# Score passes of the first query block between second value products, and key blocks 2 and 3 through one transposed tile

## The chip, the cores and the metric

One Trainium2 chip, one core. The metric is the device time of one execution in microseconds, the median of several runs. All arithmetic of the attention runs in float32, where each operand that a product needs exactly is split in a high and a low half.

## The reference

A decoder trunk of two layers on 512 tokens (plus 16 learned meta tokens in front), width 1024. Each layer has one combined input projection and two parallel mixers, a causal pooling and a latent attention with 8 heads, both gated and added:

```python
h = rmsnorm(h_res, norm_gain[l])
proj = h @ w_in[l]
u_pool, z_pool, c_q, c_kv, k_rope, z_mla, g_pool, g_mla = jnp.split(proj, IN_SPLIT_POINTS, axis=-1)
y_pool = (pool_mix(u_pool, pool_w_group[l], pool_scale[l]) * jax.nn.silu(z_pool)) @ pool_w_up[l]
o_mla = mla(c_q, c_kv, k_rope, pos, q_a_norm_gain[l], kv_a_norm_gain[l], w_q_b[l], w_kv_b[l],
            q_norm_gain[l], k_norm_gain[l])
y_mla = (o_mla * jax.nn.silu(z_mla)) @ mla_w_up[l]
merged = jax.nn.sigmoid(g_pool) * y_pool + jax.nn.sigmoid(g_mla) * y_mla
h_res = h_res + merged @ w_out[l]
```

Inside `mla`, each head computes for each block of 128 queries `softmax(q k^T * scale)` over all keys up to the block's end, and the product of these weights with the values.

## The kernel before

Activations lie transposed: features on the 128 partitions, the 528 tokens along the free axis. A plan lists every weight product of both layers in order ("Gemm"); a generator (`stream`) emits them pass by pass. Each product is three TensorE passes (`mm3`, lines 180 to 182): high by high, high by low, low by high. In layer 0 a product covers the tokens in two segments of 264 columns, in layer 1 (`self.last`), where the meta tokens are no longer wanted, in one of 512.

The attention of a layer is emitted in between. `gap()` emits so many nanoseconds (`FILL`) of the plan's passes as filler, and the loop over the 8 heads goes round like this: score passes of query blocks 1, 2 and a part of 3 of head h; gap; first part of the value products of head h-1 (key blocks 0 and 1); gap; score passes of the rest of block 3 and of block 0, row minima, exponentials and normalisation of head h; gap; `prep` of head h+1, second part of the value products of head h-1 (key blocks 2 and 3); gap.

A scheduler then sets each engine's own order when the kernel is built: among the instructions whose inputs it holds for ready, those emitted first go first. On the chip each engine follows that order; semaphores make it wait where an input is late. So filler passes that were emitted later can stand between two steps of a head whose inputs were not ready together.

The steps of one head, in the order in which one feeds the next:

- `prep`: the keys are scaled (DVE line 742, POOL line 743), and split into `kh` (ACT, line 271) and `kl` (DVE, line 272).
- `scores(i)`: `mm3` of query block i, 128 columns of weights from `qh` or `ql`, with 144 columns (block 0), 272 (1), 400 (2), and 240 and 288 (3, in two parts) of keys, into PSUM tiles "S".
- `top` (line 774): scale, mask and row minimum on DVE. `expo` (line 781): the exponential on ACT with row sum. Then the reciprocal of the row sums on DVE (line 813), and on POOL the normalisation of the weights of all four blocks (lines 818 and 820).
- `pv`, per key block j: transposes of the normalised weights (line 839), split into `th` (ACT, line 271) and `tl` (DVE, line 272), then two products into the PSUM tile "o": the wide one (line 844, 128 columns of weights with the value's high and low half, `th` moving) and the low one (line 845, 64 columns of weights, `tl` moving). Each has 512 - 128 j columns. Odd heads also turn the weights of the meta tokens (line 850).
- `part2` (line 868): the meta tokens' share, and the gate.

Of the kernel before, what the change touches and what calls it, by code (L numbers as in the profile page):

```python
# [9 lines left out]
F32 = mybir.dt.float32  # L10
F32R = mybir.dt.float32r
BF16 = mybir.dt.bfloat16
I32 = mybir.dt.int32
AF = mybir.ActivationFunctionType
# [4 lines left out]
P = 128  # L19
DEPTH = 2  # L20
D = 1024
SEQ = 512
NM = 16
# [4 lines left out]
H = 8  # L28
# [43 lines left out]
def trunk(ctx, tc, xT, xrow, mrow, pos, win, wkr, wqb, wkb, wvb, wgr, wpu, wmu, wout, gains, const, yT):  # L72
    nc = tc.nc
    pe, act, dve, gp, sp = nc.tensor, nc.scalar, nc.vector, nc.gpsimd, nc.sync
# [5 lines left out]
    sm = ctx.enter_context(tc.tile_pool(name="sm", bufs=1))  # L80
    dp = ctx.enter_context(tc.tile_pool(name="dp", bufs=1, space=bass.MemoryType.DRAM))
    pp = ctx.enter_context(tc.tile_pool(name="pp", bufs=1, space=bass.MemoryType.PSUM))
# [3 lines left out]
    def nm(s):  # L86
        uid[0] += 1
        return f"{s}_{uid[0]}"
# [10 lines left out]
    def mmt():  # L99
        return pp.tile([P, 512], F32, tag="mm", name=nm("mm"), bufs=4)  # L100

    def sct():
        return pp.tile([P, 512], F32, tag="S", name=nm("S"), bufs=3)
# [27 lines left out]
    ident = cst[:, C_ID:C_ID + P]  # L131
# [27 lines left out]
    vt = cp.tile([P, 4, H, P], F32R, name="vt")  # L159
# [109 lines left out]

    def split(hi, lo, src, a, b):  # L270
        act.activation(hi[:, a:b], src, AF.Copy)  # L271
        dve.tensor_sub(lo[:, a:b], src, hi[:, a:b].bitcast(F32))  # L272

    def behind(ins, other):
        tc.add_manual_dep(ins.ins, other.ins.name,
                          mybir.DependencyInfo(mybir.DependencyClass.Sync, mybir.DependencyReason.DATA))
# [32 lines left out]
    class Layer:  # L309
# [449 lines left out]
        def head(self, h, kq, prev):  # L759
            kh, kl, qh, ql = kq  # L760
            odd = h % 2
            nqs = self.nqs
            pa = slot("pa", bufs=2, w=416)
            pb = slot(f"cq{8 + odd}")
            pc = slot(f"cq{10 + odd}")
            bia = sm.tile([P, 5], F32, tag="bia", name=nm("bia"), bufs=2)
            rs = sm.tile([P, 5], F32, tag="rs", name=nm("rs"), bufs=2)

            def scores(i, out, a, b):
                q0 = NM + P * i  # L770
                mm3(out, qh[:, q0:q0 + P], ql[:, q0:q0 + P], kh[:, a:b], kl[:, a:b], True, True)

            def top(i, c, sv, mask):
                dve.tensor_tensor_reduce(out=sv, in0=sv, in1=mask, scale=nqs[:, i, h:h + 1], scalar=3e38,  # L774
                                         op0=ALU.add, op1=ALU.min, accum_out=bia[:, c:c + 1])

            def causal(n):
                return maskw[:, 512 - n:]

            def expo(i, c, sv, pv):  # L780
                act.activation(pv, sv, AF.Exp, scale=-1.0, bias=bia[:, i:i + 1], accum_out=rs[:, c:c + 1])  # L781

            pt = [pa[:, 0:144], pa[:, 144:416], pb[:, 0:400], pc[:, 0:T]]
            sa = sct()
            s1, s3 = sa[:, 0:272], sa[:, 272:272 + SPL]
            scores(1, s1, 0, 272)
            scores(3, s3, 0, SPL)
            top(1, 1, s1, causal(272))
            top(3, 4, s3, maskw[:, 0:SPL])
            sb = sct()  # L790
            s2 = sb[:, 0:400]
            scores(2, s2, 0, 400)
            if not self.last:
                mm3(sb[0:NM, 400:416], qh[:, 0:NM], ql[:, 0:NM], kh[:, 0:NM], kl[:, 0:NM], True, True)
                dve.tensor_add(self.smeta[:, h, :], sb[0:NM, 400:416], cst[0:NM, C_MM:C_MM + NM])
            top(2, 2, s2, causal(400))
            expo(1, 1, s1, pt[1])
            expo(2, 2, s2, pt[2])
            self.gap()
            self.pv(prev, (0, 1))  # L800
            self.gap()
            sc = sct()
            s0, s4 = sc[:, 0:144], sc[:, 144:144 + T - SPL]
            scores(3, s4, SPL, T)
            scores(0, s0, 0, 144)
            top(3, 3, s4, causal(T - SPL))
            top(0, 0, s0, causal(144))
            dve.tensor_tensor(out=bia[:, 3:4], in0=bia[:, 3:4], in1=bia[:, 4:5], op=ALU.min)  # L808
            expo(3, 4, s3, pt[3][:, 0:SPL])
            expo(3, 3, s4, pt[3][:, SPL:T])  # L810
            expo(0, 0, s0, pt[0])
            dve.tensor_add(rs[:, 3:4], rs[:, 3:4], rs[:, 4:5])
            dve.reciprocal(rs[:, 0:4], rs[:, 0:4])  # L813
            if odd == 0:
                self.pm = sm.tile([P, 4, 32], F32, tag="pm", name=nm("pm"), bufs=2)
            for i in range(4):
                n = pt[i].shape[1]
                gp.tensor_mul(self.pm[:, i, 16 * odd:16 * odd + 16], pt[i][:, 0:NM],  # L818
                              rs[:, i:i + 1].to_broadcast([P, NM]))
                gp.tensor_mul(pt[i][:, NM:], pt[i][:, NM:], rs[:, i:i + 1].to_broadcast([P, n - NM]))  # L820
            return h, pt, self.pm

        def pv(self, prev, js):
            if prev is None:
                return
            h, pt, pm = prev
            p, odd = h // 2, h % 2
            if js[0] == 0:
                self.o = sct() if h == H - 1 else pp.tile([P, 512], F32, tag="o", name=nm("o"), bufs=1)
            ops = self.o  # L830
            if odd == 1 and js[0] == 0:
                self.pmr = sm.tile([P, 4, 2, 32], F32R, tag="pmr", name=nm("pmr"))
                act.activation(self.pmr[:, :, 0, :], pm, AF.Copy)
                dve.tensor_sub(self.pmr[:, :, 1, :], pm, self.pmr[:, :, 0, :].bitcast(F32))
            for j in js:
                n = SEQ - P * j
                tr = mmt()
                for i in range(j, 4):
                    pe.transpose(tr[:, P * (i - j):P * (i - j + 1)], pt[i][:, NM + P * j:NM + P * (j + 1)], ident)  # L839
                th = tp.tile([P, W], F32R, tag="th", name=nm("th"), bufs=2)  # L840
                tl = tp.tile([P, W], F32R, tag="tl", name=nm("tl"), bufs=2)
                split(th, tl, tr[:, :n], 0, n)
                out = ops[:, P * j:512]
                pe.matmul(out, vt[:, j, h, :], th[:, :n], start=j == 0, stop=j == 3)  # L844
                pe.matmul(out[0:64], vt[:, j, h, 0:64], tl[:, :n], start=False, stop=j == 3, skip_group_check=True)  # L845
            if js[-1] != 3:
                if odd == 1:
                    tr = sct() if h == H - 1 else mmt()
                    for i in range(4):
                        pe.matmul(tr[0:64, P * i:P * (i + 1)], self.pmr[:, i].rearrange("p a b -> p (a b)"), identr,  # L850
                                  start=True, stop=True)
                    self.mt = slot("racc", F32R)
                    act.activation(self.mt[0:64, 0:512], tr[0:64, :], AF.Copy)
                    act.activation(self.mt[64:96, 0:512], tr[0:32, :], AF.Copy)
                return
            if odd == 0:
                self.op = tmp()
            n0, m0 = (64, 0) if odd else (0, 64)
            op = self.op[n0:n0 + 64, NM:T]
            act.activation(op, ops[m0:m0 + 64, :], AF.Copy)  # L860
            dve.tensor_add(op, ops[n0:n0 + 64, :], op)
            if odd == 1:
                op = self.op
                mt = self.mt

                def part2():
                    th, m = mt, mmt()
                    pe.matmul(m, self.vb[:, P * p:P * (p + 1)], th[0:96, 0:512], start=True, stop=True)  # L868
                    self.ogs[p] = (slot(f"q{p}", F32R), slot(f"kn{p}", F32R))
                    f = op[:, NM:T]  # L870
                    dve.tensor_add(f, m, f)
                    dve.tensor_mul(f, f, self.zms[p][:, NM:T])
                    split(*self.ogs[p], f, NM, T)

                after((3 if p == 3 else 2) * LAG, part2)
# [141 lines left out]
        def go(self, nxt):  # L1017
# [42 lines left out]
            prev = None  # L1060
            for h in range(H):
                kn_ = self.head(h, kq, prev)
                self.gap()
                if h + 1 < H:
                    kq = self.prep(h + 1)
                self.pv(prev, (2, 3))
                prev = kn_
                self.gap()
            fill_now(1300)
            self.pv(prev, (0, 1))  # L1070
            if not self.last:
                self.meta_queries()
            fill_now(2600)
            self.pv(prev, (2, 3))
            up("gm7")
            flush()
            if not self.last:
# [84 lines left out]
```

## Time and profile before

| | |
|---|---|
| median of three runs | 778.08 us (778.04 to 778.8) |
| the profiled execution | 778.45 us, of which the span is 776.6 us |
| TensorE busy | 771.7 us, 5251 passes |
| weight loads | 702.8 us, 5251 |
| DVE, ACT, POOL busy | 534.3, 414.2, 206.9 us |
| mean granted TensorE clock | 0.999 |
| attention of layer 0 | about 173 to 323 us into the span (first score pass to last value product) |
| attention of layer 1 | about 565 to 706 us into the span |

In the profile, PE is a TensorE pass and PEld its weight load. A row of the timeline has the start, the duration, the engine, the line, the operation, the tile written and those read, the weights' rows and columns, and the moving operand's partitions and columns. TensorE's passes overlap in its pipeline, so their durations add up to more than the time.

### The profile page before, as it was taken

What the parts mean: (1) busy time and instruction counts of PE and PEld (TensorE: products, weight loads), DVE (VectorE), ACT (ScalarE), POOL (GpSimd) and SP (SyncE); (2) the same over time, 40 slices, a digit from 0 to 9 for tenths busy, and PEclk for the clock granted to TensorE, in tenths of its full rate; (3) what the DMA queues carried; (4) which work ended last, traced back from release to release, by engine and by line L of the source; (5) the groups of instructions that cost most, each with busy time, mean ns of one, the idle gap of its engine ahead of it and who ended that gap; (6) DMA issues with size and microseconds to landing.
All of it is one profiled execution on the core that took longest, in us unless ns stands there. A gap on an engine that the chain in (4) does not pass through costs nothing.

```text
span 776.6 us, 14527 instructions
## 1 busy us (share of the span) xinstructions
PE 771.7 (99%) x5251; PEld 702.8 (90%) x5251; DVE 534.3 (69%) x1155; ACT 414.2 (53%) x930; POOL 206.9 (27%) x265
## 2 busy tenths in 40 slices
PE   9999999999999999999999999999999999999998
PEld 8999899999999999999997898887788888888887
DVE  5588688357788977785466486774577888765932
ACT  6755656545666665633354365455446666654420
POOL 1026404012334242052120263030132433420500
PEclk9999999999999999999999999999999999999999
DMA  8533234433222222325643332244232332122372
GB/s 284 164 112 98 74 92 123 123 96 103 92 82 87 79 67 71 96 82 153 188 134 91 110 89 87 79 132 141 76 123 89 96 89 89 59 79 68 108 241 85
DMA packets 54932, 84.04 MB, mean 108 GB/s; under 512 B 10007, under 2 KB 18583, under 8 KB 54861
## 3 DMA queue, kind: packets, MB, share of 16 engines
q1 hardware_dynamic: 54716, 82.86, 35.2%
q8 instruction: 41, 0.67, 0.4%
q14 instruction: 31, 0.25, 0.1%
q10 hardware_dynamic: 144, 0.26, 0.1%
HBM read 76.68 MB, written 4.29 MB: 104 GB/s over the span
## 4 chain that ended last, share of the span: by engine, by line
PE 99%; DMA 1%; SPq 0%; ACT 0%; DVE 0%; issue 0%
PE mm L180 29%; PE mm L182 29%; PE mm L181 29%; PE mm L839 2%; PE S L181 2%; PE S L182 2%; PE S L180 2%; PE o L844 1%; PE o L845 1%; PE S L498 1%; DMA raw<-win 1%; PE S L462 0%; PE mm L868 0%; PE mm L387 0%; PE mm L850 0%; PE S L845 0%
## 5 line engine op out<-in xcount | busy, mean ns | idle before, releaser
L180 PE MATMUL mm<-hh,whi 128*128 128x264 f32 (+2 forms) x1096 | 345.4, 317 | 0.3 <-ACT whi L175 0.3
L181 PE MATMUL mm<-hl,whi 128*128 128x264 f32 (+2 forms) x1096 | 343.2, 314 | 0.0
L182 PE MATMUL mm<-hh,wlo 128*128 128x264 f32 (+2 forms) x1096 | 342.5, 314 | 0.0
L176 DVE TENSOR_TENSOR wlo<-raw,whi 128x512 fp32r<-128x512 f32 (+2 forms) x251 | 181.4, 726 | 103.7 <-ACT whi L175 101.4
L175 ACT ACTIVATE whi<-raw 128x512 fp32r<-128x512 f32 (+2 forms) x251 | 150.5, 603 | 178.9 <-PE mm L181 134.3
L180 PEld LDWEIGHTS mm<-hh,whi 128*128 128x128 f32 x1096 | 205.5, 188 | 13.6 <-ACT whi L175 0.5
L181 PEld LDWEIGHTS mm<-hl,whi 128*128 128x128 f32 x1096 | 206.1, 188 | 12.0
L182 PEld LDWEIGHTS mm<-hh,wlo 128*128 128x128 f32 x1096 | 205.2, 188 | 12.2
L743 POOL TENSOR_TENSOR tmp<-kp,bc 64x528 f32<-64x528 f32 x16 | 24.8, 1552 | 103.7 <-issue 53.5
L818 POOL TENSOR_TENSOR pm<-pa,rs 128x16 f32<-128x16 f32 x32 | 11.7, 365 | 148.6 <-DVE rs L813 148.6
L604 POOL TENSOR_TENSOR racc<-racc,tmp 128x264 f32<-128x264 f32 (+1 forms) x15 | 14.3, 957 | 113.9 <-ACT tmp L603 113.9
L928 POOL TENSOR_TENSOR tmp<-tmp,xb 128x264 f32<-128x264 f32 (+1 forms) x24 | 26.7, 1134 | 57.7 <-DVE tmp L926 55.5
L774 DVE CUSTOM_DVE_ANT_0 S<-S,maskw,nqs 128x272 f32<-128x272 f32 (+4 forms) x80 | 38.4, 498 | 2.2 <-PE S L182 1.9
L180 PE MATMUL mm<-u,whi 128*128 128x264 f32 (+1 forms) x108 | 35.1, 325 | 0.0
L182 PE MATMUL mm<-u,wlo 128*128 128x264 f32 (+1 forms) x108 | 34.7, 321 | 0.0
L180 PE MATMUL mm<-cq,whi 128*128 128x264 f32 (+1 forms) x108 | 34.6, 321 | 0.0
L181 PE MATMUL mm<-cq,whi 128*128 128x264 f32 (+1 forms) x108 | 34.6, 321 | 0.0
L182 PE MATMUL mm<-cq,wlo 128*128 128x264 f32 (+1 forms) x108 | 34.6, 320 | 0.0
L272 DVE TENSOR_TENSOR tl<-mm,th 128x512 fp32r<-128x512 f32 (+1 forms) x64 | 29.3, 482 | 7.0 <-ACT th L271 6.0
L781 ACT ACTIVATE cq<-S,bia 128x400 f32<-128x400 f32 (+2 forms) x48 | 24.5, 515 | 17.8 <-DVE bia L808 8.8
L820 POOL TENSOR_TENSOR cq<-cq,rs 128x384 f32<-128x384 f32 (+1 forms) x32 | 33.5, 1047 | 0.0
L271 ACT ACTIVATE th<-mm 128x512 fp32r<-128x512 f32 (+1 forms) x64 | 25.4, 434 | 6.5 <-PE mm L839 5.9
(271 smaller groups left out, 1370.8 us busy)
## 6 DMA issues: line engine op xcount, KB each, us to landing
raw<-win SPq DMA_DIRECT2D x143, 256.0 KB, 2.6
raw<-wout SPq DMA_DIRECT2D x32, 256.0 KB, 3.0
bc<-kdr SPq DMA_DIRECT2D x16, 264.0 KB, 3.1
raw<-wpu SPq DMA_DIRECT2D x16, 256.0 KB, 2.9
raw<-wmu SPq DMA_DIRECT2D x16, 256.0 KB, 2.7
raw<-wqb SPq DMA_DIRECT2D x12, 256.0 KB, 3.0
xb<-xT SPq DMA_DIRECT2D x8, 264.0 KB, 5.5
tmp<-xT SPq DMA_DIRECT2D x16, 132.0 KB, 3.4
```

Source lines behind the costliest of these rows:

```text
L175: act.activation(hi[:, :n], raw[:, :n], AF.Copy)
L176: dve.tensor_sub(lo[:, :n], raw[:, :n], hi[:, :n].bitcast(F32))
L180: pe.matmul(out, wh, xh, start=start, stop=False)
L181: pe.matmul(out, wh, xl, start=False, stop=False)
L182: newest[0] = pe.matmul(out, wl, xh, start=False, stop=stop)
L271: act.activation(hi[:, a:b], src, AF.Copy)
L272: dve.tensor_sub(lo[:, a:b], src, hi[:, a:b].bitcast(F32))
L743: gp.tensor_mul(kf[r0:r0 + 64, :], self.kp[r0:r0 + 64, :], bc[r0:r0 + 64, :])]
L774: dve.tensor_tensor_reduce(out=sv, in0=sv, in1=mask, scale=nqs[:, i, h:h + 1], scalar=3e38, op0=ALU.add, op1=ALU.min, accum_out=bia[:, c:c ...
L781: act.activation(pv, sv, AF.Exp, scale=-1.0, bias=bia[:, i:i + 1], accum_out=rs[:, c:c + 1])
L820: gp.tensor_mul(pt[i][:, NM:], pt[i][:, NM:], rs[:, i:i + 1].to_broadcast([P, n - NM]))
L928: gp.tensor_add(t[:, :b - a], t[:, :b - a], self.am[m][:, a:b])
```

## The change

In layer 0, for every head that has a previous one, the three score passes of query block 0 are no longer emitted in a run. They go to `pv` as "hosts" of the second part of the previous head's value products. `pv` now has three parts: part 0 turns and splits key blocks 0 and 1; part 1, one gap later, has their products, with the score passes in between, and the low product of block 0 in two halves of 256 columns; part 2 has key blocks 2 and 3. In layer 1 parts 0 and 1 are emitted one behind the other, and the last head of each layer does its products in part 0; there the score passes of block 0 stay in a run.

In part 2, in both layers, the transposes of key blocks 2 and 3 go into one PSUM tile of 384 columns with one split, and the products are ordered: wide 2, wide 3, low 3, low 2.

`follow` sets an order between two instructions of an engine without a semaphore. `behind` makes an instruction wait: the first and third host wait for the low half (`tl`) of block 0's and block 1's tile, and the wide product of block 3 for that of the shared tile.

```diff
     def split(hi, lo, src, a, b):
         act.activation(hi[:, a:b], src, AF.Copy)
-        dve.tensor_sub(lo[:, a:b], src, hi[:, a:b].bitcast(F32))
+        return dve.tensor_sub(lo[:, a:b], src, hi[:, a:b].bitcast(F32))
+
+    def follow(ins, other):
+        tc.add_manual_dep(ins.ins, other.ins.name,
+                          mybir.DependencyInfo(mybir.DependencyClass.NoSync, mybir.DependencyReason.SCHED_ONLY))
...
-            self.pv(prev, (0, 1))
+            self.pv(prev, 0)
+            if self.last:
+                self.pv(prev, 1)
             self.gap()
             sc = sct()
             s0, s4 = sc[:, 0:144], sc[:, 144:144 + T - SPL]
             scores(3, s4, SPL, T)
-            scores(0, s0, 0, 144)
+            if prev is None or self.last:
+                scores(0, s0, 0, 144)
+            else:
+                q0 = slice(NM, NM + P)
+                self.pv(prev, 1, [lambda k=k, q=q, x=x: pe.matmul(s0, q[:, q0], x[:, 0:144], start=k == 0, stop=k == 2)
+                                  for k, (q, x) in enumerate(((qh, kh), (qh, kl), (ql, kh)))])
...
+            def turned(js):
+                tr, c = mmt(), 0
+                for j in js:
+                    for i in range(j, 4):
+                        pe.transpose(tr[:, c:c + P], pt[i][:, NM + P * j:NM + P * (j + 1)], ident)
+                        c += P
                 th = tp.tile([P, W], F32R, tag="th", name=nm("th"), bufs=2)
                 tl = tp.tile([P, W], F32R, tag="tl", name=nm("tl"), bufs=2)
-                split(th, tl, tr[:, :n], 0, n)
-                out = ops[:, P * j:512]
-                pe.matmul(out, vt[:, j, h, :], th[:, :n], start=j == 0, stop=j == 3)
-                pe.matmul(out[0:64], vt[:, j, h, 0:64], tl[:, :n], start=False, stop=j == 3, skip_group_check=True)
-            if js[-1] != 3:
+                return th, tl, split(th, tl, tr[:, :c], 0, c)
+
+            def ready(t, fn):
+                ins = fn()
+                behind(ins, t[2])
+                return ins
+
+            def both(j, t, c):
+                n = SEQ - P * j
+                return pe.matmul(ops[:, P * j:512], vt[:, j, h, :], t[0][:, c:c + n], start=j == 0, stop=j == 3)
+
+            def low(j, t, c, a=0, b=512):
+                a, b = max(a, P * j), min(b, 512)
+                return pe.matmul(ops[0:64, a:b], vt[:, j, h, 0:64], t[1][:, c + a - P * j:c + b - P * j],
+                                 start=False, stop=j == 3, skip_group_check=True)
+
+            def chain(*fns):
+                last = None
+                for fn in fns:
+                    ins = fn()
+                    if last is not None:
+                        follow(ins, last)
+                    last = ins
+
+            if part == 0:
+                self.t01 = [turned((0,)), turned((1,))]
+            if part == (0 if final else 1):
+                t0, t1 = self.t01
+                if hosts:
+                    chain(lambda: both(0, t0, 0), lambda: ready(t0, hosts[0]), lambda: low(0, t0, 0, 0, 256), hosts[1],
+                          lambda: low(0, t0, 0, 256, 512))
+                    chain(lambda: both(1, t1, 0), lambda: ready(t1, hosts[2]), lambda: low(1, t1, 0))
+                else:
+                    for j, t in enumerate(self.t01):
+                        both(j, t, 0)
+                        low(j, t, 0)
...
+            if part < 2:
                 return
+            t = turned((2, 3))
+            chain(lambda: both(2, t, 0), lambda: ready(t, lambda: both(3, t, 256)), lambda: low(3, t, 256), lambda: low(2, t, 0))
...
-                self.pv(prev, (2, 3))
+                self.pv(prev, 2)
...
-            self.pv(prev, (0, 1))
+            self.pv(prev, 0)
...
-            self.pv(prev, (2, 3))
+            self.pv(prev, 2)
```

More of the change, by code (lines that the diff above doesn't have):

```diff
@@ L821, in head, with pv @@
             return h, pt, self.pm
-        def pv(self, prev, js):
+        def pv(self, prev, part, hosts=()):
             if prev is None:
@@ L827, in pv @@
             p, odd = h // 2, h % 2
-            if js[0] == 0:
-                self.o = sct() if h == H - 1 else pp.tile([P, 512], F32, tag="o", name=nm("o"), bufs=1)
-            ops = self.o
[L831 to L839, printed above, removed]
+            final = h == H - 1
@@ new lines, in pv @@
+            if part == 0:
+                self.o = sct() if final else pp.tile([P, 512], F32, tag="o", name=nm("o"), bufs=1)
+                if odd == 1:
+                    self.pmr = sm.tile([P, 4, 2, 32], F32R, tag="pmr", name=nm("pmr"))
+                    act.activation(self.pmr[:, :, 0, :], pm, AF.Copy)
+                    dve.tensor_sub(self.pmr[:, :, 1, :], pm, self.pmr[:, :, 0, :].bitcast(F32))
+            ops = self.o
+            def turned(js):
[4 more added lines that the diff above has]
+                        c += P
@@ new lines, in chain @@
+            def chain(*fns):
[5 more added lines that the diff above has]
+                    last = ins
+            if part == 0:
+                self.t01 = [turned((0,)), turned((1,))]
[9 more added lines that the diff above has]
+                        low(j, t, 0)
@@ L847, in pv @@
                 if odd == 1:
-                    tr = sct() if h == H - 1 else mmt()
+                    tr = sct() if final else mmt()
                     for i in range(4):
```

## The prediction

> **What bounds the kernel now.** I read the page first (span, clock, chain), then TensorE's passes in order of time inside the attention stretch of layer 0, then its weight loads over the same microseconds, and last the vector, scalar and GpSimd engines between one head and the next.
>
> ```profile
> span 776.6 us, 14527 instructions
> PE 771.7 (99%) x5251; PEld 702.8 (90%) x5251; DVE 534.3 (69%) x1155; ACT 414.2 (53%) x930; POOL 206.9 (27%) x265
> PEclk9999999999999999999999999999999999999999
> PE 99%; DMA 1%; SPq 0%; ACT 0%; DVE 0%; issue 0%
> ```
>
> TensorE is busy in 99% of the span, the chain that ends last is TensorE for 99% of its length, and the granted clock is full in every slice. So the time is the sum of what TensorE's passes cost, one behind the other, and an edit is worth what it changes in that sum, plus any wait that it brings to TensorE. The durations in these rows are no prices, because passes overlap in the pipeline: the price of a pass is the distance from its start to the next start. Here are the three score passes of query block 0 (144 columns) of one head, between wide passes:
>
> ```profile
> 211.88 0.28 PE L182 MATMUL mm<-hh,wlo 128*128 128x264 f32 x1
> 212.00 0.23 PE L180 MATMUL S<-kh,qhl 128*128 128x144 f32 x1
> 212.06 0.28 PE L181 MATMUL S<-kl,qhl 128*128 128x144 f32 x1
> 212.17 0.28 PE L182 MATMUL S<-kh,qhl 128*128 128x144 f32 x1
> 212.29 0.33 PE L180 MATMUL mm<-hh,whi 128*128 128x264 f32 x1
> 212.45 0.29 PE L181 MATMUL mm<-hl,whi 128*128 128x264 f32 x1
> 212.58 0.39 PE L844 MATMUL o<-th,vt 128*128 128x512 f32 x1
> 212.81 0.28 PE L182 MATMUL mm<-hh,wlo 128*128 128x264 f32 x1
> ```
>
> A 264-column pass costs 0.12 us (211.88 to 212.00) and a 512-column pass 0.23 (212.58 to 212.81). The difference, 0.11 us for 248 columns, is 0.444 ns a column. By that a 144-column pass should cost 0.12 - 120 x 0.000444 = 0.067 us and a 128-column pass 0.06. But the second and third score passes take 0.11 and 0.12, and the wide pass behind them 0.16 (212.29 to 212.45) in place of 0.12. The weight loads of the same stretch say why:
>
> ```profile
> 212.00 0.19 PEld L181 LDWEIGHTS S<-kl,qhl 128*128 128x128 f32 x1
> 212.11 0.19 PEld L182 LDWEIGHTS S<-kh,qhl 128*128 128x128 f32 x1
> 212.22 0.19 PEld L180 LDWEIGHTS mm<-hh,whi 128*128 128x128 f32 x1
> 212.33 0.19 PEld L181 LDWEIGHTS mm<-hl,whi 128*128 128x128 f32 x1
> ```
>
> The load for the next pass starts when the present pass starts (212.00 in both views), and loads of 128 columns follow each other at 0.11 us. So a pass costs the larger of its own stream and the load of the pass behind it. A 264-column pass (0.12) covers that load; a 144-column pass (0.067) does not. Three short passes in a row take 0.33 us of loads (212.00 to 212.33) for 0.20 of streams: 0.13 us a head lost.
>
> The same loss, smaller, sits at the last value products (key block 3, 128 columns):
>
> ```profile
> 222.46 0.28 PE L845 MATMUL o<-tl,vt 128*64 128x256 f32 x1
> 222.58 0.22 PE L844 MATMUL o<-th,vt 128*128 128x128 f32 x1
> 222.64 0.22 PE L845 MATMUL o<-tl,vt 128*64 128x128 f32 x1
> 222.70 0.34 PE L181 MATMUL mm<-hl,whi 128*128 128x264 f32 x1
> 222.87 0.28 PE L182 MATMUL mm<-hh,wlo 128*128 128x264 f32 x1
> ```
>
> ```profile
> 222.64 0.19 PEld L181 LDWEIGHTS mm<-hl,whi 128*128 128x128 f32 x1
> 222.75 0.19 PEld L182 LDWEIGHTS mm<-hh,wlo 128*128 128x128 f32 x1
> ```
>
> The wide product (222.58) is followed by the low product after 0.06 us: it is not delayed, because the low product loads only 64 columns, and 0.06 covers that. The low product itself (222.64) is followed by a pass with 128 columns of weights. The next loads are 0.11 apart, and the pass behind takes 0.17 in place of 0.12. So 0.05 us is lost behind every 128-column product whose successor loads 128 columns.
>
> **The change part by part.**
>
> *Score passes of query block 0 between value products.* This holds in layer 0 for heads 1 to 7; head 0 and all of layer 1 keep the run of three. The new order is: wide product of block 0 (512 columns), score pass, low product's first half (256), score pass, low product's second half (256); then wide product of block 1 (384), score pass, low product (384). Each score pass's 128-column load lies under a pass of 256 columns or more (at least 0.117 us by the slope, against 0.11), and behind each score pass (0.067) comes a 64-column load, which 0.06 covers. All 0.13 us are won back: 7 x 0.13 = 0.91 us.
>
> ```profile
> 282.17 0.28 PE L182 MATMUL S<-kh,qhl 128*128 128x144 f32 x1
> 282.29 0.40 PE L850 MATMUL mm<-identr,pmr 128*64 128x128 f32 x4
> ```
>
> In one of the seven heads the third pass already has a pass with 64 columns of weights behind it, so I take 0.04 (0.11 less 0.067) off: 0.87.
>
> The split low product adds one pass a head. Two of 256 columns cost 2 x 0.117 = 0.234 against 0.23, some 0.005 us, in all 0.04. Net of this part: 0.83 us.
>
> The interleaved run itself is not in the trace. Its bounds are that every score pass still pays 0.11 (nothing won, 0.04 lost) and that it costs 0.06, the shortest start-to-start of the rows above (another 21 x 0.007 = 0.15 won). I take the covered price of 0.067, since the row that is nearest, a 128-column product in front of a 64-column load, shows exactly its stream.
>
> *Key blocks 2 and 3 through one tile.* Both layers, all heads. The order becomes wide block 2 (256), wide block 3 (128), low block 3 (128), low block 2 (256). Behind both 128-column products there is now a 64-column load, and the last pass, 256 columns, covers a load of 128.
>
> ```profile
> L845 PE MATMUL o<-tl,vt 128*64 128x128 f32 x14 | 3.2, 229 | 0.0
> L845 PE MATMUL S<-tl,vt 128*64 128x128 f32 x2 | 0.4, 221 | 0.0
> ```
>
> ```profile
> 204.56 0.22 PE L844 MATMUL o<-th,vt 128*128 128x128 f32 x1
> 204.62 0.33 PE L180 MATMUL mm<-hh,whi 128*128 128x264 f32 x1
> ...
> 706.32 0.22 PE L844 MATMUL S<-th,vt 128*128 128x128 f32 x1
> ```
>
> All 16 low products of block 3 lose 0.05 now. In five heads (the first and the last are shown) the wide product loses it too, because another pass stands between it and its low product. 21 x 0.05 = 1.05 us. If the new pairs were pulled apart by wide passes, all 32 would lose it, 0.55 us more than now; if the gain is not a stall's doing it cannot be above 1.05. I take 1.05, as 11 of the 16 pairs stand together today and the new wait on the split's second half stands in front of the pair, not inside it.
>
> *What is moved at no price.* The transposes are the same in number and place. The products of blocks 0 and 1 stand one filler stretch later, with the plan's filler passes in between, so the cover is the wide passes that the rows above show on both sides; were they used up, TensorE would wait for the split tiles. Sixteen copies and sixteen subtractions of splits are saved on engines that the chain does not name. No DMA is issued or moved, and neither SP's nor POOL's queue is passed.
>
> *The added wait.* The first and the third hosted score pass wait for the vector engine's low half of the tile. The low product behind each needs that half anyway, so TensorE gets no new wait of its own, but the score of block 0 comes later. Behind it stand the row minimum on the vector engine, the exponentials, and the normalisation on GpSimd. What that does is the second rival.
>
> *A rule against this.* The rows show a load starting with the previous pass, both with all 128 rows. The Trainium skill, "TensorE: Matmul & The Clock Gate", Part 3 (What overlaps and what doesn't), says that weight loads overlap running matmuls only where the row group differs. By that rule no order of these passes could hide a load; the loads at 212.00 and 222.64 contradict it here.
>
> The sum: 0.83 + 1.05 = 1.88, so 1.9 us less. The profiled execution (778.45, of which 776.6 is the span) would become 776.6. It stands 0.37 above the median of the three runs, 778.08, and the forecast goes from the median: **776.2 us**. A difference of 0.2% (1.56 us) is about what a measurement of this kernel can tell from no change.
>
> **The rivals.**
>
> *First: the groups do not stay together.* If wide passes slip in behind each score pass and behind each product of block 3, 0.87 of the gain is gone, the 0.04 of the split remain, and block 3 costs 0.55 more: 778.1 + 0.6 = 778.7. Against it: in the rows above passes that become ready together are issued together. For it: five pairs are apart today.
>
> *Second, slower: the later score reaches the next head.* In one head of the trace the whole chain runs without slack:
>
> ```profile
> 215.14 0.34 PE L845 MATMUL o<-tl,vt 128*64 128x384 f32 x1
> ...
> 223.37 0.58 PE L180 MATMUL S<-kh,qhl 128*128 128x272 f32 x2
> ```
>
> ```profile
> 212.06 1.14 DVE L272 TENSOR_TENSOR tl<-mm,th 128x512 fp32r<-128x512 f32 x2
> ...
> 213.72 0.38 DVE L774 CUSTOM_DVE_ANT_0 S<-S,maskw,nqs 128x144 f32<-128x144 f32 x1
> ```
>
> ```profile
> 219.57 1.59 POOL L820 TENSOR_TENSOR cq<-cq,rs 128x512 f32<-128x512 f32 x1
> 221.12 1.52 POOL L743 TENSOR_TENSOR tmp<-kp,bc 64x528 f32<-64x528 f32 x1
> 232.92 1.81 POOL L743 TENSOR_TENSOR tmp<-kp,bc 64x528 f32<-64x528 f32 x1 [10.28 <-issue]
> ...
> 241.44 1.04 POOL L820 TENSOR_TENSOR cq<-cq,rs 128x512 f32<-128x512 f32 x1
> ```
>
> ```profile
> 222.68 0.64 ACT L271 ACTIVATE kh<-tmp 128x528 fp32r<-128x528 f32 x1 [3.41 <-POOL tmp L743]
> ```
>
> The low halves are done by 213.20, but TensorE comes to the low product of block 1 only at 215.14, since its order is fixed. The third hosted score pass stands just ahead of that product, so the minimum over block 0 starts at about 215.14 + 0.28 = 215.42 (the row's place plus a score pass's 0.28 to its end) and not at 213.72: 1.7 us later. GpSimd normalises this head and only then makes the next head's key (221.12, straight behind 219.57). The scalar engine then finishes it at 223.32, and TensorE reads it at 223.37. There are 0.05 us of slack, so TensorE would wait 1.65 us. In the next head GpSimd makes the key ahead of the normalisation (232.92 before 241.44), and the delay reaches no score pass. One such head costs 1.65 and leaves 776.2 + 1.65 = 777.85, within 0.2%. Three cost 4.95: **781.1 us**. It decides from the third head on, since (1.88 + 1.56) / 1.65 is 2.1.
>
> *Third: loads cannot be hidden.* If each load ran by itself, the order of passes would be worth nothing, and the seven added passes would cost a 64-column load (0.06) more each: 778.1 + 7 x 0.06 = 778.5. This is what the rule quoted above would give. The loads that start with a running pass speak against it.
>
> **How the numbers follow.** Forecast as summed, up to a few tenths lost to single pulled-apart pairs: 0.55, with its own range 775.8 to 776.5. One or two heads waiting: 0.17 (777.85 for one). Groups pulled apart: 0.06 (778.7). Loads not hidden: 0.02 (778.5). Three heads or more waiting: 0.20 (781.1). Faster by over 0.2% is the first, 0.55; within it the next three, 0.25; slower the last, 0.20. The low end, 775.8, is the forecast less the 0.15 of the lower bound and 0.25 for the spread of the runs (from 778.04 to 778.08 and 778.8); the high end, 778.8, takes in the rivals within 0.2% and leaves out the 0.20 above.
>
> **What would show it.** Right: the hosted score passes 0.07 before a low product and no load pair 0.11 apart there; behind the low product of block 2 a pass at its normal 0.12; span near 774.7. Wrong: wide passes between a score pass and its low product; idle before TensorE's first score passes of a head, released by the scalar engine's key; GpSimd's key product always behind the normalisations; the attention stretch of layer 0 longer than before.

## The result, and the profile after

The changed kernel is slower by a little: 779.8 us against 778.47, a ratio of 1.0017 with a 95% interval of 1.001 to 1.0023. The profiled execution took 779.65 us (778.45 before), its span 777.7 us (776.6). The forecast of 776.2 and its range, 775.8 to 778.8, both missed, and on the other side of no change.

The same lines of the page of the kernel after as were shown of before (span; busy time of each engine; granted clock; the chain that ended last):

```profile
span 777.7 us, 14480 instructions
PE 771.6 (99%) x5258; PEld 702.6 (90%) x5258; DVE 533.0 (69%) x1139; ACT 411.1 (53%) x914; POOL 205.2 (26%) x265
PEclk9999999999999999999999999999999999999999
PE 95%; DVE 2%; ACT 1%; DMA 0%; POOL 0%; issue 0%; SPq 0%; ACTq 0%; DVEq 0%; POOLq 0%
```

The counts are as announced: 7 passes more (the split low products), 16 subtractions and 16 activations fewer. The clock is still full. The chain is new: 3% of it now belongs to the vector and scalar engines. So TensorE waits, which it hardly did before.

TensorE's passes after, in time, in one head of layer 0. These are the hosted score passes (line 815) between the value products (line 865 wide, 869 low):

```profile
248.42 0.39 PE L865 MATMUL o<-th,vt 128*128 128x512 f32 x1
248.65 0.23 PE L815 MATMUL S<-kh,qhl 128*128 128x144 f32 x1
248.71 0.28 PE L869 MATMUL o<-tl,vt 128*64 128x256 f32 x1
248.84 0.23 PE L815 MATMUL S<-kl,qhl 128*128 128x144 f32 x1
248.90 0.28 PE L869 MATMUL o<-tl,vt 128*64 128x256 f32 x1
249.02 0.33 PE L865 MATMUL o<-th,vt 128*128 128x384 f32 x1
```

And key block 3, both of its products between wider passes:

```profile
276.64 0.22 PE L865 MATMUL o<-th,vt 128*128 128x128 f32 x1
276.71 0.34 PE L869 MATMUL o<-tl,vt 128*64 128x128 f32 x2
276.88 0.29 PE L182 MATMUL S<-kh,qhl 128*128 128x272 f32 x1
```

Each hosted pass shown costs 0.06 (248.65 to 248.71, 248.84 to 248.90), and the low product behind it is not late. Of all 21 hosted passes, 18 cost 0.064 to 0.071 and one 0.080. The third of two heads (at 214.58 and 249.43) costs 0.117 and 0.116: the short turns of the meta weights (line 895) stand right ahead of it, so its own load is not hidden. The pair of low products of blocks 3 and 2 takes 0.17 (276.71 to 276.88), which is 0.06 and 0.12 with nothing lost. That much went as predicted. The waits are elsewhere. This view lists who waited for whom, for TensorE's weight loads between 160 and 345 us (us in total, times, longest). For the kernel before, the same view has no row.

```profile
PEld S L180 <- ACT cq L785: 1.0, 1, 1.0
PEld mm L852 <- DVE tmp L919: 0.9, 1, 0.9
PEld o L865 <- ACT th L271: 0.5, 2, 0.3
PEld mm L180 <- DVE tmp L621: 0.4, 1, 0.4
```

**How the two effects are told apart.** The distances between the starts of TensorE's passes fit the prediction's price rule closely. A stream of N columns takes 0.4435 N + 4.9 ns (264 columns: 122 ns; 512: 232). The load of the next pass takes 110 ns for 128 columns and 57 for 64. Over all passes of a stretch, what the load takes beyond the stream is summed as *load loss*, and what a distance takes beyond both as *waits*, a net remainder (distances below the rule subtract). The stretches are 160 to 345 us (layer 0's attention) and 562 to 718 us (layer 1's). Every kernel of this study, in us:

| kernel | median | ratio to before, 95% | layer 0: load loss, waits | layer 1: load loss, waits |
|---|---|---|---|---|
| before | 778.47 | | 6.49, 0.33 | 5.15, 0.25 |
| after | 779.8 | 1.0017 (1.001 to 1.0023) | 5.36, 3.35 | 4.62, 0.02 |
| `shared_only` | 779.38 | 1.001 (1.0001 to 1.0019) | 6.05, 2.37 | 4.62, 0.00 |
| `hosts_only` | 779.08 | 1.0007 (0.9998 to 1.0016) | 5.74, 0.97 | 5.15, 0.24 |
| `hosts_no_wait` | 780.28 | 1.0018 (1.0009 to 1.0027) | 5.56, 3.32 | 4.62, 0.01 |
| `before_f2900` | 779.58 | 1.0017 (1.0008 to 1.0026) | 6.60, 1.45 | 5.15, 0.26 |
| `before_f2925` | 778.32 | 1.0004 (0.9993 to 1.0015) | 6.40, 0.35 | 5.15, 0.26 |
| `before_f2975` | 779.91 | 1.0016 (1.0004 to 1.0029) | 6.56, 1.48 | 5.15, 0.23 |
| `before_f3000` | 781.5 | 1.0038 (1.0023 to 1.0053) | 6.40, 3.20 | 5.15, 0.24 |
| `after_f2900` | 778.59 | 0.9999 (0.9989 to 1.0008) | 5.36, 2.32 | 4.62, 0.02 |
| `after_f2925` | 777.76 | 0.9995 (0.9983 to 1.0006) | 5.33, 1.42 | 4.62, 0.02 |
| `after_f2975` | 779.44 | 1.0015 (1.0004 to 1.0026) | 5.33, 3.04 | 4.62, 0.02 |
| `after_f3000` | 779.26 | 1.0009 (1.0 to 1.0019) | 5.41, 2.90 | 4.62, 0.02 |
| `pmr_last` | 776.92 | 0.9982 (0.9973 to 0.9991) | 5.44, 0.38 | 4.72, 0.10 |
| `pmr_last_f2925` | 777.23 | 0.9986 (0.9977 to 0.9995) | 5.36, 0.85 | 4.72, 0.12 |
| `shared_pmr_last` | 782.77 | 1.0057 (1.0042 to 1.0072) | 6.10, 3.77 | 4.72, 0.10 |
| `before_pmr_last` | 784.18 | 1.0081 (1.0064 to 1.0098) | 6.56, 5.96 | 5.25, 0.02 |

Load losses and waits come from one profiled execution of each kernel, medians and ratios from all its runs; the ratio is to runs of the kernel before on the same chip. For the change: loads 1.13 + 0.53 = 1.66 less, waits 3.02 more in layer 0 and 0.23 less in layer 1, the split's 0.04: 1.17 in all, against the spans' 1.1. Outside the two stretches the kernels before and after keep step. The table's profiled executions are not all typical: those of `shared_only` and `before_f2975` lost some 1.6 us more in the first 20 us, which the columns leave out, and that of `shared_pmr_last` (780.61 us) lies 2.2 below its median.

**Where TensorE waits after.** Two of the places, in TensorE's order of time:

```profile
263.56 0.28 PE L181 MATMUL mm<-hl,whi 128*128 128x264 f32 x1
264.56 0.33 PE L852 MATMUL mm<-cst,pa 128*128 128x128 f32 x1 [0.72 <-DVE tmp L919]
...
282.74 0.29 PE L182 MATMUL S<-kh,qhl 128*128 128x288 f32 x1
283.82 0.39 PE L180 MATMUL S<-kh,qhl 128*128 128x272 f32 x1 [0.79 <-ACT cq L785]
```

A pass due 0.12 to 0.13 later starts 1.00 and 1.08 later: 0.88 and 0.95 of waits. The first is a transpose that needs a PSUM tile that the vector engine still reads (line 919, where `part2` adds the meta tokens' share). The second is the first score pass of head 7, which needs the PSUM tile whose exponential (line 785) is late. Beside them stand 0.7 at 266 to 267 us, a third of it for `th` on the scalar engine and the rest at a pass that waits for a vector product (line 621), and 0.28 at 257 us, for `th` too.

The second wait can be followed back. The vector engine after, then the scalar engine, over the same microseconds:

```profile
278.22 0.77 DVE L845 TENSOR_TENSOR pmr<-pm,pmr 128x128 fp32r<-128x128 f32 x1 [1.41 <-ACT pmr L844]
279.00 1.73 DVE L746 TENSOR_TENSOR tmp<-kn,bc 64x528 f32<-64x528 f32 x1
280.77 0.51 DVE L778 CUSTOM_DVE_ANT_0 S<-S,maskw,nqs 128x272 f32<-128x272 f32 x1
...
282.37 0.63 DVE L778 CUSTOM_DVE_ANT_0 S<-S,maskw,nqs 128x400 f32<-128x400 f32 x1
```

```profile
277.88 0.31 ACT L844 ACTIVATE pmr<-pm 128x128 fp32r<-128x128 f32 x1 [1.52 <-POOL pm L829]
...
283.08 0.59 ACT L785 ACTIVATE cq<-S,bia 128x400 f32<-128x400 f32 x1
```

Read from below: the exponential at 283.08 frees the tile for 283.82. It waits for the row minimum at 282.37. The score passes of that minimum had started by 277.70, so it could have come over four microseconds earlier. But in the vector engine's order the subtraction of the meta tokens' weights (`pmr`, line 845, needed by TensorE only at 288.8) stands ahead of all three minima. It sits 1.41 us idle for the scalar engine's copy, which sits 1.52 idle for GpSimd's normalisation (`pm`). Behind it comes a key product (line 746), and then the minima. The same head on the vector engine before:

```profile
274.48 0.50 DVE L774 CUSTOM_DVE_ANT_0 S<-S,maskw,nqs 128x272 f32<-128x272 f32 x1
...
275.08 0.48 DVE L774 CUSTOM_DVE_ANT_0 S<-S,maskw,nqs 128x240 f32<-128x240 f32 x1
...
275.80 0.77 DVE L834 TENSOR_TENSOR pmr<-pm,pmr 128x128 fp32r<-128x128 f32 x1 [0.19 <-ACT pmr L833]
276.58 1.75 DVE L742 TENSOR_TENSOR tmp<-kn,bc 64x528 f32<-64x528 f32 x1
...
279.16 0.64 DVE L774 CUSTOM_DVE_ANT_0 S<-S,maskw,nqs 128x400 f32<-128x400 f32 x1
```

There two of the minima go first, and the subtraction then waits 0.19. The third minimum, whose tile head 7 needs, stands behind the subtraction and the key product in both kernels; it comes 3.2 us later after (279.16 and 282.37). The subtraction starts 2.4 later because GpSimd's last `pm` product does, before and then after:

```profile
275.21 0.21 POOL L818 TENSOR_TENSOR pm<-cq,rs 128x16 f32<-128x16 f32 x1
```

```profile
277.63 0.21 POOL L829 TENSOR_TENSOR pm<-cq,rs 128x16 f32<-128x16 f32 x1
```

The two other minima now stand between, which is most of the rest. No instruction was added here; the change altered the order that was fixed when the kernel was built, and made `pm` later. How much of that lateness comes from TensorE's waits at 264 to 267 us, and how much from the later score of block 0, is not separated.

### The profile page after: what moved, and what is told of

Its sections match the earlier page's. It is cut to its first block, busy times and chain, and to the rows that moved or that the text cites. A ratio compares the mean times of both kernels' runs of the same rounds, so it can differ in the third digit from the quotient of the medians.

```text
span 777.7 us, 14480 instructions
## 1 busy us (share of the span) xinstructions
PE 771.6 (99%) x5258; PEld 702.6 (90%) x5258; DVE 533.0 (69%) x1139; ACT 411.1 (53%) x914; POOL 205.2 (26%) x265
## 4 chain that ended last, share of the span: by engine, by line
PE 95%; DVE 2%; ACT 1%; DMA 0%; POOL 0%; issue 0%; SPq 0%; ACTq 0%; DVEq 0%; POOLq 0%
PE mm L180 28%; PE mm L182 28%; PE mm L181 28%; PE mm L852 2%; PE S L180 2%; PE S L181 2%; PE S L182 2%; PE o L869 1%; PE o L865 1%; PE S L502 1%; PE S L466 0%; DVE wlo L176 0%; DMA xb<-xT 0%; DVE S L778 0%; DVE xb L623 0%; DVE tmp L746 0%
## 5 line engine op out<-in xcount | busy, mean ns | idle before, releaser
L176 DVE TENSOR_TENSOR wlo<-raw,whi 128x512 fp32r<-128x512 f32 (+2 forms) x251 | 183.9, 736 | 106.7 <-ACT whi L175 101.4
L272 DVE TENSOR_TENSOR tl<-mm,th 128x384 fp32r<-128x384 f32 (+1 forms) x48 | 28.0, 593 | 6.8 <-ACT th L271 6.4
L181 PE MATMUL mm<-kn,whi 128*128 128x264 f32 (+1 forms) x88 | 28.5, 325 | 0.0
```

Of the source, the lines that this page charges most:

```text
L176: dve.tensor_sub(lo[:, :n], raw[:, :n], hi[:, :n].bitcast(F32))
L181: pe.matmul(out, wh, xl, start=False, stop=False)
L272: return dve.tensor_sub(lo[:, a:b], src, hi[:, a:b].bitcast(F32))
```

## The experiments

**Each part alone.** `shared_only` keeps the shared tile and drops the hosts:

```diff
-            if self.last:
-                self.pv(prev, 1)
+            self.pv(prev, 1)
...
-            if prev is None or self.last:
-                scores(0, s0, 0, 144)
-            else:
...
+            scores(0, s0, 0, 144)
```

> Only key blocks 2 and 3 are changed (one tile, new order); block 0's score passes stay in a run in both layers. The gain by the loads is 1.05 us. Delay theory (TensorE waits because the hosted score passes come later): no waits over those of before, so about 777.4 us. Shared-tile theory (the waits come from the one split of blocks 2 and 3): the 3 us of waits stay, about 780.4. Order theory (the waits belong to one particular order of the engines' queues, and any edit deals anew): anything from 777.4 to 780.4, with the waits in other heads.

`hosts_only` keeps the hosts and splits blocks 2 and 3 as before:

```diff
-            t = turned((2, 3))
-            chain(lambda: both(2, t, 0), lambda: ready(t, lambda: both(3, t, 256)), lambda: low(3, t, 256), lambda: low(2, t, 0))
+            for j in (2, 3):
+                t = turned((j,))
+                both(j, t, 0)
+                low(j, t, 0)
```

> Only the score passes of block 0 are moved between the value products (layer 0); key blocks 2 and 3 keep their two tiles and the old order. The gain by the loads is 0.8 us. Delay theory: about 3 us of waits in heads 5 to 7 of layer 0, so 780.5. Shared-tile theory: no new waits, 777.7. Order theory: waits between 0 and 3 us, in other heads than in the full change.

The load losses split as the parts do. The hosts alone save 0.75 (6.49 to 5.74), predicted 0.87; the shared tile alone saves 0.44 + 0.53 = 0.97, predicted 1.05. Both kernels wait more than before all the same (0.64 us more in layer 0 for the hosts alone, 2.04 for the shared tile alone), so neither part alone is at fault. In `shared_only`, without a hosted pass, the vector engine shows the very order of the changed kernel, first this row, then the minimum:

```profile
278.85 0.77 DVE L839 TENSOR_TENSOR pmr<-pm,pmr 128x128 fp32r<-128x128 f32 x1 [1.42 <-ACT pmr L838]
...
282.01 0.49 DVE L778 CUSTOM_DVE_ANT_0 S<-S,maskw,nqs 128x272 f32<-128x272 f32 x1
```

TensorE waits some 1.9 us between 283 and 287 us there, 0.7 of it at head 7's first score pass. So a hosted score of block 0 is not needed for this wait. Nor is it enough: in `hosts_only` that head's normalisation starts 1.5 us later than before (273.96 against 272.47), but all three minima stand ahead of the subtraction, and head 7's first score pass does not wait.

**The added wait away.** `hosts_no_wait` takes the two waits off the hosted passes (the low products keep theirs):

```diff
-lambda: ready(t0, hosts[0]),
+hosts[0],
...
-lambda: ready(t1, hosts[2]),
+hosts[2],
```

> The full change, but the first and third hosted score pass do not wait for the split's low half (the low products behind them still do, by their data). Delay theory: block 0's score comes earlier, the waits shrink to under 1 us, about 777.0 with 0.04 us lost where a wide pass slips in behind a score pass. Shared-tile theory: waits unchanged, about 779.8. Order theory: anything from 776.6 to 780.

The time stays (1.0018), and so do the waits: 3.32 us, with the same two rows on top of the view of who waited for whom.

```profile
PEld S L180 <- ACT cq L785: 1.0, 1, 1.0
PEld mm L852 <- DVE tmp L919: 0.9, 1, 0.9
```

The edit is a weak test of the delay. In the head at 268 us the first hosted pass came at 267.58 in place of 268.84, but the third, which completes the score, came at 270.00 in place of 269.88.

**Another order, the change untouched.** The filler between the steps of a head was set from 2950 to four other values, in the kernel after and in the kernel before. The work is the same; only the order of the queues moves.

```diff
-FILL = (2950.0, 2850.0)
+FILL = (2925.0, 2850.0)
```

> The full change with 2900 in place of 2950 ns of filler in each gap of layer 0: the same instructions, a slightly different order. Delay theory: with less time in each gap the heads are tighter, waits of 3 us or more, 779.8 or above. Order theory: the waits change by microseconds either way without a rule; 776.6 to 781.

> The full change with 2925 ns of filler in each gap of layer 0. Order theory: the load gain is as in the full change, TensorE's waits in layer 0 lie anywhere from 0.3 to 3.5 us (776.7 to 780). Delay theory: between the waits at 2900 (2.3 us) and at 2950 (3.3 us).

> The full change with 2975 ns. Order theory: waits anywhere from 0.3 to 3.5 us. Delay theory: between those at 2950 (3.3) and 3000 (2.9).

> The full change with 3000 ns of filler in each gap of layer 0. Delay theory: more time in each gap, waits well below 3 us, 777 to 778.5. Order theory: waits change without a rule, 776.6 to 781.

> The kernel before with 2900 ns of filler in each gap of layer 0. Delay theory: the old order has slack, waits stay under 0.5 us, 778.5. Order theory: the kernel before sits at a lucky value, and waits of 1 to 3 us appear here too, 779.5 to 781.5.

> The kernel before with 2925 ns. Order theory: waits of 1 to 3 us (779 to 781), since the 0.3 us at 2950 are an exception and not the rule. Delay theory: waits between 0.3 and 1.5 us, below those of the full change at the same filler.

> The kernel before with 2975 ns. Order theory: waits of 1 to 3 us (779 to 781). Delay theory: below those of the full change at the same filler.

> The kernel before with 3000 ns of filler in each gap of layer 0. Delay theory: waits under 0.5 us, 778.5. Order theory: waits of 1 to 3 us, 779.5 to 781.5.

The load losses hardly move (6.40 to 6.60 before, 5.33 to 5.41 after). The waits in layer 0 go from 0.33 to 3.20 us before and from 1.42 to 3.35 after, and the places differ from kernel to kernel (at 2975 and 3000, 1.0 to 1.6 us of both kernels' waits stand at 342 to 345 us, some 20 us behind the attention). Who waited for whom, for the weight loads of `before_f3000`, then of `after_f2925`:

```profile
PEld mm L180 <- ACT hh L271: 1.0, 1, 1.0
PEld mm L839 <- DVE cq L917: 0.6, 1, 0.6
```

```profile
PEld mm L180 <- DVE cq L965: 0.9, 1, 0.9
```

Two things follow. Waits of one to three microseconds come from the order alone, and the kernel before had a nearly free one at 2950. It had another at 2925 (0.35), where 1 to 3 us had been expected by the order theory. At equal filler the kernel after has the lower ratio at 2900 (0.9999 against 1.0017), 2925 (0.9995 against 1.0004), 2975 (1.0015 against 1.0016, no difference) and 3000 (1.0009 against 1.0038). The intervals lie apart at 3000 only; at 2900 they touch. The mean over the five fillers is 1.0015 before and 1.0007 after. But the waits after are larger in four of five: 2.61 on average against 1.36. Whether the changed steps themselves make waits likelier, or five orders are too few, is open.

**The link in the vector queue moved.** `pmr_last` is the kernel after, with the meta weights' copy and subtraction ordered behind the exponential and the row minimum of block 2 of the next head. No wait is added; it is an order on the engine alone.

```diff
-            top(2, 2, s2, causal(400))
+            t2 = top(2, 2, s2, causal(400))
...
-            expo(2, 2, s2, pt[2])
+            self.tops = t2, expo(2, 2, s2, pt[2])
...
-                    act.activation(self.pmr[:, :, 0, :], pm, AF.Copy)
-                    dve.tensor_sub(self.pmr[:, :, 1, :], pm, self.pmr[:, :, 0, :].bitcast(F32))
+                    follow(act.activation(self.pmr[:, :, 0, :], pm, AF.Copy), self.tops[1])
+                    follow(dve.tensor_sub(self.pmr[:, :, 1, :], pm, self.pmr[:, :, 0, :].bitcast(F32)), self.tops[0])
```

> The full change; in addition the meta weights' copy (scalar engine) and subtraction (vector engine) of odd heads are ordered behind the row minimum and the exponential of query block 2 of the head in work. Queue theory (the vector engine waits 1.4 us for these weights ahead of three row minima, whose PSUM tiles TensorE then waits for): the 0.95 us wait at head 7's first score pass goes, with it the vector engine's waits at this subtraction; waits in layer 0 fall from 3.35 to 2.4 us or less, 778.8 or below. Order theory without this cause: waits anywhere from 0.3 to 3.5 us and the vector engine as late as before.

> The same at 2925 ns of filler. The full change has 1.42 us of waits there, of which 0.33 at head 7's first score pass. Queue theory: about 1.1 us of waits, 777.4. Order theory: 776.5 to 779.7.

776.92 us, and 777.23 with the other filler: both beat the kernel before (0.9982, 0.9986) and the kernel after. The vector engine of `pmr_last` in the same head, then TensorE, then its page:

```profile
275.42 0.51 DVE L778 CUSTOM_DVE_ANT_0 S<-S,maskw,nqs 128x272 f32<-128x272 f32 x1 [0.61 <-PE S L182]
...
278.12 0.62 DVE L778 CUSTOM_DVE_ANT_0 S<-S,maskw,nqs 128x400 f32<-128x400 f32 x1
...
280.27 0.28 DVE L845 TENSOR_TENSOR pmr<-pm,pmr 128x128 fp32r<-128x128 f32 x1
```

```profile
280.95 0.30 PE L182 MATMUL S<-kh,qhl 128*128 128x288 f32 x1
281.09 0.29 PE L180 MATMUL S<-kh,qhl 128*128 128x272 f32 x1
```

```profile
span 775.0 us, 14477 instructions
PE 99%; DMA 0%; ACT 0%; DVE 0%; SPq 0%; issue 0%; ACTq 0%
```

The minima come first, released by TensorE itself, and head 7's first score pass follows 0.14 behind its predecessor in place of 1.08. The key product, now ahead of the subtraction, also takes 0.81 us (276.59) in place of 1.73. The waits fall from 3.35 to 0.38, and the span, 1.6 below that of before, is the load gain of 1.48 (1.05 + 0.43) and 0.10 of waits. The wait at 264 us went too; why that one did was not followed.

The same order without the hosts and without the whole change, `shared_pmr_last` and `before_pmr_last`:

> Only key blocks 2 and 3 changed, with the meta weights ordered behind the row minimum. Queue theory: of its 2.37 us of waits the ones between 283 and 287 us (1.8 us) go, so 0.3 to 0.6 remain and 777.5 us. Order theory: waits from 0.3 to 3.3, 777.4 to 780.4.

> The kernel before, with the meta weights ordered behind the row minimum as in pmr_last. If the gain of pmr_last comes from the change's hidden loads, this kernel stays at the time of before (0.33 us of waits leave nothing to win), 778.3 us, or gets slower by an order's waits, up to 781. If the ordering itself were worth 1.7 us, it would reach 777.

Both are slower, 1.0057 and 1.0081, and above every time expected for them. Who waited for whom, for the weight loads of `before_pmr_last`:

```profile
PEld o L849 <- DVE tl L272: 2.3, 2, 1.7
PEld mm L854 <- DVE pmr L838: 1.0, 1, 1.0
```

Here the order falls badly in an earlier odd head, at 210 to 215 us: the low product of block 0 and the passes on the meta weights wait. So the order is no gain in itself, and what `pmr_last` gains is the change's load loss. It also weakens the proof: an order imposed at one place shuffles the rest, so that `pmr_last` shows the wait at 283 us to be removable in this way, and the change to be a gain without such waits, but not that this link alone was worth all 3 us.

## Why the prediction was wrong

- **What bounds the kernel, and the price of a pass: right.** The rule of stream or load explains the load losses of every kernel in the table.
- **Hosted passes and shared tile: right in kind, a little large.** 0.87 + 1.05 = 1.92 of load loss forecast, 1.66 measured. Two hosted passes behind the turns of the meta weights are 0.10 of the difference.
- **What is moved at no price: this step failed.** It said that the passes of blocks 0 and 1 move under cover of filler, and that the vector and scalar engines may be left out since the chain does not name them. The wide filler passes are there, but cover is a matter of each queue's order. TensorE's waits in layer 0 rose from 0.33 to 3.35 us, more than the whole forecast gain of 1.88. The chain of before does not name these engines because its order was a nearly free one, which the fillers show: the same kernel has 0.35, 1.45, 1.48 and 3.20 us of waits at the other values.
- **The added wait: no new wait of TensorE from it, as said.** Taking it away changed nothing, though that test was weak. What the step named as next, a later score of block 0, did occur. The start of GpSimd's normalisation of head 1, before and then after:

```profile
198.92 0.22 POOL L818 TENSOR_TENSOR pm<-pa,rs 128x16 f32<-128x16 f32 x1 [9.35 <-DVE rs L813]
```

```profile
200.96 0.25 POOL L829 TENSOR_TENSOR pm<-pa,rs 128x16 f32<-128x16 f32 x1 [5.79 <-DVE rs L824]
```

- **The second rival: right place, wrong link.** It put the loss at the next head's first score pass, by way of GpSimd's key. The normalisation is 2.0 us later in head 1 (forecast 1.7) and 2.3 in head 2, yet TensorE waits for neither, and `pmr_last` has the same delay (201.00) without waits. The wait that did come at that pass, 0.95 us in head 7, runs through a PSUM tile, the row minima and a subtraction that stood ahead of them for want of `pm`. GpSimd's normalisation was late there too, so the rival's first link may have a part in it; the order of the vector engine was not in it. The rival's "three heads or more" did not happen; four single waits at different places did.
- **The first and third rivals: wrong.** All 21 hosted passes and all 16 pairs of block 3 are followed by a low product, as built, and the loads are hidden: otherwise the order of the passes could not have taken 1.66 us off the load loss. The Trainium skill's rule in "TensorE: Matmul & The Clock Gate", Part 3, that loads overlap only where the row group differs, is against the measured 0.06 of a hosted pass with all 128 rows.
- **The range** ended at 778.8, 1.0 below the result. It held no case for the order as such, though moving steps in a kernel whose order is fixed ahead redraws it. By the five fillers of the kernel before, that is worth 0.33 to 3.20 us of waits, as large as the gain.

## What to carry to other kernels

Where short TensorE passes stand in a row, put each in front of a narrow weight load, with its own load under a wide pass; the saving can be summed from start-to-start distances and holds. But where each engine's order is fixed when the kernel is built, any move redraws all the orders: look in the queues of the other engines for an instruction that waits ahead of work that TensorE needs sooner, and move that too. Measure before and after at several settings that only reshuffle the order, since one setting compares two draws as much as two kernels.

## What the runs showed of the hardware that was not expected

A cluster of waits can cost the clock as well. Stretches of `before_pmr_last` (start and end, length, busy time and count of TensorE, weight loads, vector, scalar and GpSimd engines, granted clock, DMA share, GB/s), and a pair of its passes:

```profile
210.00:215.00 5.00, 2.71 (x12) 1.29 (x11) 4.58 (x16) 3.44 (x12) 0.00 (x0) 0.78 0.40 128
215.00:219.00 4.00, 4.00 (x21) 4.00 (x21) 0.34 (x2) 1.87 (x6) 2.83 (x8) 0.50 0.02 4
```

```profile
216.11 0.42 PE L181 MATMUL mm<-hl,whi 128*128 128x264 f32 x1
216.33 0.42 PE L182 MATMUL mm<-hh,wlo 128*128 128x264 f32 x1
```

With TensorE busy for 2.71 of 5 us, the granted clock fell to 0.50 for the next 4 us, and a 264-column pass cost 0.22 in place of 0.12. By these rows some 2 of the kernel's 6 us of "waits" are clock, an estimate (half of 4 us at half speed). The single waits of about 1 us in the changed kernel left the clock full. Nor must a cluster cost it: in the profiled execution of `shared_pmr_last` TensorE was busy for 2.24 us between 210 and 215, and the clock was 1.00 there and in the 4 us behind. That execution took 780.61 us; the kernel's three others had granted clocks of 0.996 to 0.998 and took 782.64 to 783.28.

The key product of line 746 took 1.73 us at 279.00, against some 0.70 in the other seven heads (252.25 below); the kernel before has it at 276.58, with 1.75. The earlier row, and then GpSimd's work beside the later one:

```profile
252.25 0.70 DVE L746 TENSOR_TENSOR tmp<-kn,bc 64x528 f32<-64x528 f32 x1
```

```profile
277.81 1.04 POOL L831 TENSOR_TENSOR cq<-cq,rs 128x512 f32<-128x512 f32 x1
278.80 1.36 POOL L747 TENSOR_TENSOR tmp<-kp,bc 64x528 f32<-64x528 f32 x1
```

The Trainium skill, "GPSIMD Engine Reference" (the table of the engine's properties, SBUF interfaces), says that GpSimd shares its SBUF interface with VectorE and contends with vector instructions of two SBUF inputs. This product has two, and the rows agree. The subtraction of line 845 shows it too: 0.77 us at 278.22, where GpSimd is at work, and 0.28 in `pmr_last` at 280.27, where it is not. The vector engine is not always the one that loses: at 218.64 the key product took 0.71 and the 128x128 product that GpSimd began at the same time took 0.96, against 0.39 or 0.40 in six other heads.
